# Low halves of projection weights made by accumulating DMAs, two tiles ahead, in a two-block transformer kernel

## Chip, cores and metric

The kernel runs on one core of a Trainium2 chip. The metric is the device time of one execution in microseconds (us). TensorE does the matrix products, ScalarE (ACT), VectorE (DVE) and GpSimd (POOL) the elementwise work, and SyncE (SP) issues the loads.

## What is computed

Two blocks work on one sequence of 256 frames of width 1024. The change lies in the RWKV-7 mixer of the second. Its three large projections take the mixed inputs through three 1024 x 1024 weight matrices in float32:

```python
xx = jnp.pad(h, ((0, 0), (1, 0), (0, 0)))[:, :-1] - h
xs = h[None] + xx[None] * mu[:, None, None, :]
rkv = jnp.einsum('pbtd,pde->pbte', xs[:3], w_rkv)
r, k, v = rkv[0], rkv[1], rkv[2]
...
y = _wkv7_scan(r_h, heads(decay), k_h, v_h, kk, kk * heads(a).astype(f32))
```

The scan is done in chunks: small Gram matrices of the decayed keys and receptances, a triangular elimination, and a chain of four windows.

## The kernel before

Every large product is made in three passes over split operands. A weight tile of 128 x 1024 numbers is cut by `split` into a high half (ACT copies it to fp32r) and a low half (the weight minus the high half). `mm3` then issues three matmuls, on L227, L228 and L229; the low half of the weight is first needed by the third of them for keys and receptance (L229) and by the second for values (L228).

```python
act.copy(hv, src)
lo.tensor_tensor(out=lv, in0=src, in1=hv.bitcast(F32), op=ALU.subtract)
```

The engine of the subtraction, `lo`, is DVE or POOL, by a string of letters in the table `KP` (`rk`, `rr`, `rv` for the key, receptance and value weights). There are 24 such tiles in the mixer: 8 of keys (`k_proj`, four calls, profile names wk, wkh, wkl), 8 of receptance (`r_proj`, wr, wrh, wrl) and 8 of value (`v_proj`, wv, wvh, wvl). Before, all 8 key tiles, 5 receptance tiles and 5 value tiles are subtracted on DVE, and 3 receptance and 3 value tiles on POOL.

Halves live in a pool `wp` of two buffers, raw weights in a pool `wr` of two buffers of 8 KB per partition. One load on SP brings a pair of key or receptance tiles (256 columns, 1 MB); value weights come 512 KB at a time. A load starts when its raw buffer is free, that is when both its tiles have been split; a split starts when the halves two tiles back have been used by TensorE.

The tile framework orders each engine's queue by its own estimate of when an instruction can run, and each engine works its queue in order. So in the profile some instructions stand earlier than in the code (the first key split runs while the layer before still multiplies).

In the mixer TensorE goes through the key projection with the low-rank products between (until 714 us of the span), two receptance calls, the normalisation of the keys (`scale_ab`, L1390 to L1401, with the small inverse square root of L284 to L282 ahead of it), 32 x 32 Gram blocks (`blocks`, L1458), and then a filler `dense()` that holds the rest of the receptance projection, the first half of the value projection, the large Gram matrices (`gram`, evicted by DVE in L1473) and transposes (`turn_bk`), while DVE and POOL run the elimination of 15 steps (L918, L921, L924) on two halves, POOL having the products of the second half (L921). From 791 us on TensorE alternates the rest of the value projection with the products that use the elimination's result.

Of the kernel before, what the change touches and what calls it, by code (L numbers as in the profile page):

```python
# [10 lines left out]
F32 = mybir.dt.float32  # L11
F32R = mybir.dt.float32r
I32 = mybir.dt.int32
AF = mybir.ActivationFunctionType
# [3 lines left out]
P = 128  # L18
# [42 lines left out]
def _pack(d):  # L61
# [46 lines left out]
    'pv': 3,  # L108
    'r3': 'p',
    'rho': 'd',  # L110
    'rk': 'dd,dd,dd,dd',
    'rr': 'dp,pd,dd,pd',
    'rv': 'd,d,d,p,d,d,p,p',
    'sev': 2,
    'sn': 'aapd',
    'srw': 5,
# [17 lines left out]
def tile_two_blocks(ctx: ExitStack, tc: tile.TileContext, a: dict):  # L134
# [1 line left out]
    act, dve, pool, pe, sync = nc.scalar, nc.vector, nc.gpsimd, nc.tensor, nc.sync  # L136

    cp = ctx.enter_context(tc.tile_pool(name="const", bufs=1))
    EN = {"d": dve, "p": pool, "a": act}

    def scale_by(e, out, in_, cols):
        if e is act:
# [35 lines left out]

    def raw(name):
        wpick[1] += 1  # L180
        w_ = extra[-1][1] if extra and wpick[1] % 2 and not wpick[2] else wr
        return w_.tile([P, 2048], F32, tag="raw", name=name)

    def load_ws(w, c0, name, n=256):
        t = raw(name)
        v = t[:, :NK * n].rearrange("p (k c) -> p k c", k=NK)
        sync.dma_start(out=v, in_=w[:, c0:c0 + n].rearrange("(k p) c -> p k c", p=P))
        return v
# [16 lines left out]
    def split(src, name, lo=dve, at=None):  # L205
        shape = list(src.shape)
        n = 1
        for s in shape[1:]:
            n *= s
        if at is None:  # L210
            wpick[0] += 1
            w_ = extra[-1][0] if extra and wpick[0] % 2 and not wpick[2] else wp
            h = w_.tile([P, 1024], F32R, tag="wh", name=name + "h")
            l = w_.tile([P, 1024], F32R, tag="wl", name=name + "l")
        else:
            x = area(at, [2, D], F32R)
            h, l = x[:, 0], x[:, 1]
        hv, lv = h[:, :n], l[:, :n]
        if len(shape) == 3:
            hv = hv.rearrange("p (a b) -> p a b", a=shape[1])  # L220
            lv = lv.rearrange("p (a b) -> p a b", a=shape[1])
        act.copy(hv, src)  # L222
        lo.tensor_tensor(out=lv, in0=src, in1=hv.bitcast(F32), op=ALU.subtract)  # L223
        return hv, lv

    def mm3(out, lh, ll, rh, rl, first, last):
# [916 lines left out]
    def rwkv(fed, early, cols, mu, hcol, hka, laf):  # L1143
        NP, CH = 8, 64
        half = 0.5 * DECAY
        with tc.tile_pool(name="rw", bufs=1) as bp:
            nkeep = _O2["reset2"][0]
            cc = bp.tile([P, nkeep], F32, tag="cc2", name="cc2")
            sync.dma_start(out=cc, in_=a["c2"][:, :nkeep])
# [41 lines left out]
            with tc.tile_pool(name="rwm2", bufs=2) as m2, tc.tile_pool(name="rwm", bufs=1) as mp:  # L1191
# [9 lines left out]
                xx = xxf.rearrange("p (k t) -> p k t", k=NK)  # L1201
                mixf = m2.tile([P, 2, 1024], F32, tag="mix", name="mix", bufs=1)
                sqf = m2.tile([P, 2, 512], F32, tag="sq", name="sq", bufs=1)
                w3 = a["rwkv_w_rkv_2"][0]

                xh, xl, _, part = fed
                pool.memset(hT[:, :, 0:1], 0.0)
# [78 lines left out]
                nk = mp.tile([P, 2, 2 * NP], F32, tag="nk", name="nk")  # L1286

                def k_proj(c, kh, kl):
                    w = load_ws(w3[1], c * 256, f"wk{c}")
                    hl = [split(w[:, :, j * P:(j + 1) * P], "wk", EN[KP["rk"].split(",")[c][j]]) for j in range(2)]  # L1290
                    q = lin("k")
                    qv = q.rearrange("p (j t) -> p j t", j=2)
                    if c == 0:
                        for i, j, k in [(i, j, k) for i in range(2) for j in range(2) for k in range(4 * i, 4 * i + 4)]:
                            mm3(qv[:, j], hl[j][0][:, k], hl[j][1][:, k], kh[:, k], kl[:, k],
                                (i, j, k) == (0, 0, 0), (i, j, k) == (1, 1, 7))
                    else:
                        for j in range(2):
                            ws(qv[:, j], *hl[j], kh, kl)
                    s = slice(2 * c, 2 * c + 2)  # L1300
                    act.copy(tK[:, s], as4(qv))
                    if KP["ka"][c] == "a":
                        for j in range(2):
                            act.activation(out=tA[:, 2 * c + j], in_=as2(qv)[:, j], func=AF.Copy,
                                           scale=cols[:, 64 + 2 * c + j:65 + 2 * c + j])
                    else:
                        dve.tensor_tensor(out=tA[:, s], in0=as2(qv), in1=cols[:, 64 + 2 * c:66 + 2 * c].unsqueeze(2)
                                          .unsqueeze(3).to_broadcast([P, 2, 2, P]), op=ALU.mult)
                    sq = sqf[:, c % 2].rearrange("p (j t) -> p j t", j=2)
                    act.activation(out=as2(sq), in_=tA[:, s], func=AF.Square)  # L1310
                    q = ps("kk")
                    for t in range(2):
                        for j in range(2):
                            pe.matmul(q[:, 4 * t + 2 * j:4 * t + 2 * j + 2], lhsT=sq[:, j, t * P:(t + 1) * P],
                                      rhs=cst("par"), start=True, stop=True)
                    dve.tensor_scalar(nk[:, :, 4 * c:4 * c + 4], q[:, :8].rearrange("p (t k) -> p t k", t=2),
                                      1e-24, RS, ALU.max, ALU.mult)
# [83 lines left out]
                    EN[KP["tk"][1]].tensor_tensor(out=tK[:, s], in0=tK[:, s], in1=as4(tt[:, s]), op=ALU.mult)  # L1401

                def r_proj(c):
                    w = load_ws(w3[0], c * 256, f"wr{c}")
                    q = lin("r")
                    qv = q.rearrange("p (j t) -> p j t", j=2)
                    for j in range(2):
                        wh, wl = split(w[:, :, j * P:(j + 1) * P], "wr", EN[KP["rr"].split(",")[c][j]])
                        for k in range(NK):
                            mm3(qv[:, j], wh[:, k], wl[:, k], rh[:, k], rl[:, k], k == 0, k == NK - 1)  # L1410
                            if k % 2:
                                yield 1
                    s = slice(2 * c, 2 * c + 2)
                    dve.tensor_mul(as4(pr[:, s]), as4(qv), tK[:, s])
                    dve.tensor_tensor(out=tR[:, s], in0=as4(qv), in1=EL5[:, s, :, :, 1:], op=ALU.mult)
                    EN[KP["tt"]].tensor_tensor(out=tK[:, s], in0=tK[:, s], in1=as4(EnL[:, s]), op=ALU.mult)
# [92 lines left out]
                def v_proj(n):  # L1509
                    ac = gv[2]  # L1510
                    m = slice(n * 512, n * 512 + 512)
                    for c in range(4):
                        w = raw(f"wv{n}{c}")[:, :1024].rearrange("p (k c) -> p k c", k=2)
                        sync.dma_start(out=w, in_=w3[2][c * 256:c * 256 + 256, m].rearrange("(k p) c -> p k c", p=P))
                        wh, wl = split(w, "wv", EN[KP["rv"].split(",")[4 * n + c]])
                        for j in range(2):
                            k = 2 * c + j
                            for t in range(2):
                                s = slice(t * P, t * P + P)
                                mm3(ac[t][:, m], vh[:, k, s], vl[:, k, s], wh[:, j], wl[:, j], k == 0, k == NK - 1)  # L1520
                                yield k, t
# [276 lines left out]
                    add_res(ac[1], 1, n, None)  # L1798
                for n in range(2):
                    fed[2](1, n)  # L1800
            return fed

    with more_weights(1, 1):
# [88 lines left out]
```

## Time and profile before

| | us |
|---|---|
| median of 3 runs | 1083.26 (1081.01 to 1083.73) |
| the profiled execution | 1082.76 |
| its span in the trace | 1081.0 |
| TensorE busy in the span | 1044.6 |
| DVE busy | 734.9 |
| ACT busy | 553.0 |
| POOL busy | 71.2 |

The profiled execution is 0.50 us under the median, and 1.76 us of it lie outside the span. Busy time of TensorE is modelled and matmuls overlap, so a busy TensorE is not one at its peak. In the rows below PE is TensorE's matmuls and PEld its weight loads; a wait is put down to the instruction that released it.

### The profile page before, as it was taken

What the parts mean: (1) busy time and instruction counts of PE and PEld (TensorE: products, weight loads), DVE (VectorE), ACT (ScalarE), POOL (GpSimd) and SP (SyncE); (2) the same over time, 40 slices, a digit from 0 to 9 for tenths busy, and PEclk for the clock granted to TensorE, in tenths of its full rate; (3) what the DMA queues carried; (4) which work ended last, traced back from release to release, by engine and by line L of the source; (5) the groups of instructions that cost most, each with busy time, mean ns of one, the idle gap of its engine ahead of it and who ended that gap; (6) DMA issues with size and microseconds to landing.
All of it is one profiled execution on the core that took longest, in us unless ns stands there. A gap on an engine that the chain in (4) does not pass through costs nothing.

```text
span 1081.0 us, 19651 instructions
## 1 busy us (share of the span) xinstructions
PE 1044.6 (97%) x8138; PEld 936.9 (87%) x8138; DVE 734.9 (68%) x1269; ACT 553.0 (51%) x826; POOL 71.2 (7%) x100
## 2 busy tenths in 40 slices
PE   8999999999999999999999999989999999999996
PEld 6899879988889999889999998989768869999985
DVE  5889675555568876676675556998954785555565
ACT  4745464454456454455554446852445645444452
POOL 3100000000002000000000001044320000000000
PEclk9999999999999999999999999998998999999999
DMA  8353196655564656555586541332133244665541
GB/s 245 122 157 118 45 343 196 195 162 189 160 211 139 215 157 194 160 172 185 156 273 194 179 154 47 98 105 92 60 99 112 86 156 158 193 195 187 187 133 40
DMA packets 113910, 169.44 MB, mean 157 GB/s; under 512 B 6446, under 2 KB 92443, under 8 KB 113564
## 3 DMA queue, kind: packets, MB, share of 16 engines
q1 hardware_dynamic: 113674, 168.11, 48.4%
q8 instruction: 64, 1.05, 0.4%
q14 instruction: 26, 0.21, 0.1%
q10 hardware_dynamic: 146, 0.07, 0.0%
HBM read 167.12 MB, written 1.05 MB: 156 GB/s over the span
## 4 chain that ended last, share of the span: by engine, by line
PE 82%; DVE 12%; ACT 3%; issue 2%; DMA 1%; POOL 1%; ACTq 0%; POOLq 0%; DVEq 0%
PE m1a L227 3%; PE m3h L228 3%; PE m3h L229 3%; PE m1a L229 3%; PE m1a L228 3%; PE m3h L227 3%; PE m1h L228 3%; PE m2h L228 3%; PE m2h L229 3%; PE m1h L229 3%; PE m1h L227 3%; PE m2h L227 3%; PE m2a L227 3%; PE m2a L228 3%; PE m2a L229 3%; PE m3a L227 3%
## 5 line engine op out<-in xcount | busy, mean ns | idle before, releaser
L227 PE MATMUL m1h<-m1xh,m1uh 128*128 128x256 f32 x256 | 73.4, 287 | 0.0
L229 PE MATMUL m3h<-m3xh,m3ul 128*128 128x256 f32 x256 | 72.3, 283 | 0.5 <-DVE m3ul L223 0.5
L228 PE MATMUL m3h<-m3xl,m3uh 128*128 128x256 f32 x256 | 72.2, 282 | 0.3 <-DVE m3xl L387 0.3
L227 PE MATMUL m3h<-m3xh,m3uh 128*128 128x256 f32 x256 | 72.1, 282 | 0.0
L228 PE MATMUL m1h<-m1xl,m1uh 128*128 128x256 f32 x256 | 71.9, 281 | 0.2 <-DVE m1xl L387 0.2
L229 PE MATMUL m2h<-m2xh,m2ul 128*128 128x256 f32 x256 | 71.7, 280 | 0.0
L229 PE MATMUL m1h<-m1xh,m1ul 128*128 128x256 f32 x256 | 71.7, 280 | 0.0
L228 PE MATMUL m2h<-m2xl,m2uh 128*128 128x256 f32 x256 | 71.7, 280 | 0.0
L223 DVE TENSOR_TENSOR m3ul<-m3u,m3uh 128x1024 fp32r<-128x1024 f32 x32 | 39.2, 1226 | 47.6 <-ACT m3uh L222 47.6
L227 PE MATMUL m2h<-m2xh,m2uh 128*128 128x256 f32 x256 | 71.6, 280 | 0.0
L223 DVE TENSOR_TENSOR m1ul<-m1u,m1uh 128x1024 fp32r<-128x1024 f32 x32 | 39.2, 1225 | 44.8 <-ACT m1uh L222 44.8
L223 DVE TENSOR_TENSOR m2ul<-m2u,m2uh 128x1024 fp32r<-128x1024 f32 x32 | 39.1, 1225 | 35.9 <-ACT m2uh L222 35.9
L222 ACT CAST m3uh<-m3u 128x1024 fp32r<-128x1024 f32 x32 | 33.5, 1047 | 53.9 <-PE m3h L228 50.0
L222 ACT CAST m1uh<-m1u 128x1024 fp32r<-128x1024 f32 x32 | 33.7, 1053 | 52.1 <-PE m1h L228 50.4
L222 ACT CAST m2uh<-m2u 128x1024 fp32r<-128x1024 f32 x32 | 33.5, 1050 | 47.9 <-PE m2h L228 45.4
L223 DVE TENSOR_TENSOR m2dl<-m2d,m2dh 128x1024 fp32r<-128x1024 f32 x32 | 39.2, 1224 | 26.1 <-ACT m2dh L222 26.1
L223 DVE TENSOR_TENSOR m3dl<-m3d,m3dh 128x1024 fp32r<-128x1024 f32 x31 | 38.0, 1225 | 24.9 <-ACT m3dh L222 24.9
L223 DVE TENSOR_TENSOR m1dl<-m1d,m1dh 128x1024 fp32r<-128x1024 f32 x31 | 37.9, 1224 | 22.0 <-ACT m1dh L222 22.0
L222 ACT CAST m2dh<-m2d 128x1024 fp32r<-128x1024 f32 x32 | 33.6, 1050 | 33.4 <-PE m2a L229 29.9
L222 ACT CAST m1dh<-m1d 128x1024 fp32r<-128x1024 f32 x31 | 32.5, 1047 | 35.3 <-PE m1a L229 24.4
L227 PE MATMUL m2a<-m2dh,m2fh 128*128 128x512 f32 x128 | 50.1, 391 | 0.0
L228 PE MATMUL m2a<-m2dl,m2fh 128*128 128x512 f32 x128 | 49.9, 390 | 0.0
(709 smaller groups left out, 3528.0 us busy)
## 6 DMA issues: line engine op xcount, KB each, us to landing
m1u<-in_w_up_dram SPq DMA_DIRECT2D x16, 1024.0 KB
m1d<-in_w_down_dram SPq DMA_DIRECT2D x16, 1024.0 KB, 4.9
m2u<-in_ffn_w_dram SPq DMA_DIRECT2D x16, 1024.0 KB, 6.6
m2d<-in_ffn_w_dram SPq DMA_DIRECT2D x16, 1024.0 KB, 5.6
m3u<-in_ffn_w_dram SPq DMA_DIRECT2D x16, 1024.0 KB, 5.6
m3d<-in_ffn_w_dram SPq DMA_DIRECT2D x16, 1024.0 KB, 4.8
win<-in_w_in_dram SPq DMA_DIRECT2D x10, 1024.0 KB
sv<-in_sgu_w_in_dram SPq DMA_DIRECT2D x8, 1024.0 KB, 6.9
```

What stands on the lines that cost most here:

```text
L222: act.copy(hv, src)
L223: lo.tensor_tensor(out=lv, in0=src, in1=hv.bitcast(F32), op=ALU.subtract)
L227: pe.matmul(out, lhsT=lh, rhs=rh, start=first, stop=False)
L228: pe.matmul(out, lhsT=lh, rhs=rl, start=False, stop=False)
L229: pe.matmul(out, lhsT=ll, rhs=rh, start=False, stop=last)
```

## The change

20 of the 24 weight tiles get the letter x. For them `split` no longer subtracts: ACT writes the high half, then ACT writes its negative into the low half's buffer, and POOL issues a DMA that adds the raw weights (SBUF to SBUF, 512 KB) onto it. The four key tiles of the first two calls stay on DVE. A second pool `wz` with two buffers for halves is opened around the mixer, so that halves alternate between four buffers, and `tile_of` makes each tile two tiles before TensorE uses it (one tile before in the first key call). Loads change in shape: key and receptance pairs come as two DMAs of 128 columns (512 KB each) into one raw buffer, value tiles as pairs in one load of 1 MB instead of two of 512 KB. The raw buffers stay two. The space that is reserved for descriptors of POOL's DMAs falls from the default to 1024 bytes per partition.

```diff
-    'rk': 'dd,dd,dd,dd',
-    'rr': 'dp,pd,dd,pd',
-    'rv': 'd,d,d,p,d,d,p,p',
+    'rk': 'dd,dd,xx,xx',
+    'rr': 'xx,xx,xx,xx',
+    'rv': 'x,x,x,x,x,x,x,x',
...
         act.copy(hv, src)
-        lo.tensor_tensor(out=lv, in0=src, in1=hv.bitcast(F32), op=ALU.subtract)
+        if lo == "x":
+            act.activation(out=lv, in_=hv.bitcast(F32), func=AF.Copy, scale=-1.0)
+            pool.dma_start(out=lv.bitcast(F32), in_=src, accum_op=ALU.add)
+        else:
+            lo.tensor_tensor(out=lv, in0=src, in1=hv.bitcast(F32), op=ALU.subtract)
...
+        with tc.tile_pool(name="wz", bufs=2) as wz, tc.tile_pool(name="rw", bufs=1) as bp:
+            extra.append((wz, None))
...
+            def prep(i):
+                if i > 23 or i in made:
+                    return
+                m, u = divmod(i, 8)
+                if u % 2 == 0:
+                    t = raw(f"w{'krv'[m]}{u}")
+                    if m < 2:
+                        v = t.rearrange("p (j k c) -> p j k c", j=2, k=NK)
+                        for j in range(2):
+                            sync.dma_start(out=v[:, j], in_=w3[1 - m][:, (u + j) * P:(u + j + 1) * P]
+                                           .rearrange("(k p) c -> p k c", p=P))
+                        src[i], src[i + 1] = v[:, 0], v[:, 1]
...
+                made[i] = split(src.pop(i), "w" + "krv"[m], EN[how[m][u]])
+
+            def tile_of(m, u, ahead=2):
+                for i in range(8 * m + u + ahead + 1):
+                    prep(i)
+                return made[8 * m + u]
...
-                    w = load_ws(w3[1], c * 256, f"wk{c}")
-                    hl = [split(w[:, :, j * P:(j + 1) * P], "wk", EN[KP["rk"].split(",")[c][j]]) for j in range(2)]
+                    hl = [tile_of(0, 2 * c + j, 2 if c else 1) for j in range(2)]
...
-                        wh, wl = split(w[:, :, j * P:(j + 1) * P], "wr", EN[KP["rr"].split(",")[c][j]])
+                        wh, wl = tile_of(1, 2 * c + j)
...
-                        wh, wl = split(w, "wv", EN[KP["rv"].split(",")[4 * n + c]])
+                        wh, wl = tile_of(2, 4 * n + c)
...
-    nc = bacc.Bacc("TRN2", target_bir_lowering=False, num_devices=1)
+    nc = bacc.Bacc("TRN2", target_bir_lowering=False, num_devices=1, dynamic_dma_scratch_size=1024)
```

## Rows read from the trace of the kernel before

**Rows 1.** Page, part 1: busy us (share of the span) and instructions of each engine
```profile
PE 1044.6 (97%) x8138; PEld 936.9 (87%) x8138; DVE 734.9 (68%) x1269; ACT 553.0 (51%) x826; POOL 71.2 (7%) x100
```

**Rows 2.** Stretches of 10 us: length, busy (instructions) by engine, clock, DMA share, GB/s
```profile
700.00:710.00 10.00, 9.19 (x66) 8.98 (x65) 10.00 (x17) 7.69 (x12) 4.15 (x3) 0.83 0.34 105
...
740.00:750.00 10.00, 8.66 (x88) 8.51 (x76) 9.96 (x19) 2.10 (x2) 8.02 (x6) 0.83 0.14 48
...
780.00:790.00 10.00, 9.29 (x56) 6.43 (x54) 9.44 (x25) 4.90 (x7) 1.22 (x2) 0.86 0.18 52
...
sum 120.00, PE 110.43 PEld 97.27 DVE 106.50 ACT 60.13 POOL 36.27; mean PE 9.20 PEld 8.11 DVE 8.88 ACT 5.01 POOL 3.02
```

**Rows 3.** Waits of PE, 690 to 800 us: us in total, times, longest
```profile
PE A L1469 <- DVE lx L1473: 2.4, 1, 2.4
PE nk L1394 <- ACT ly L1390: 1.6, 1, 1.6
PE AB L1458 <- issue: 1.3, 1, 1.3
PE v L227 <- DVE V L1529: 1.3, 2, 0.7
PE kk L1314 <- ACT sq L1310: 1.1, 1, 1.1
PE r L229 <- POOL wrl L223: 0.9, 1, 0.9
PE k L229 <- DVE wkl L223: 0.8, 1, 0.8
```

**Rows 4.** Groups by line, 690 to 800 us: busy us, mean ns, idle before
```profile
L223 DVE TENSOR_TENSOR wrl<-wr,wrh 128x1024 fp32r<-128x1024 f32 x5 | 6.7, 1336 | 0.0
L223 DVE TENSOR_TENSOR wvl<-wv,wvh 128x1024 fp32r<-128x1024 f32 x5 | 6.0, 1206 | 0.0
L223 DVE TENSOR_TENSOR wkl<-wk,wkh 128x1024 fp32r<-128x1024 f32 x4 | 4.8, 1212 | 0.0
...
L222 ACT CAST wrh<-wr 128x1024 fp32r<-128x1024 f32 x8 | 8.4, 1046 | 16.4 <-PE r L228 12.9 <-PE k L228 3.5
...
L223 POOL TENSOR_TENSOR wvl<-wv,wvh 128x1024 fp32r<-128x1024 f32 x3 | 7.2, 2413 | 7.8 <-ACT wvh L222 7.8
L223 POOL TENSOR_TENSOR wrl<-wr,wrh 128x1024 fp32r<-128x1024 f32 x3 | 7.1, 2369 | 11.8 <-ACT wrh L222 6.5 <-PE AB L1458 5.3
```

**Rows 5.** Timeline of DVE and of POOL around 720 us: start, us, instruction
```profile
720.08 2.31 DVE L275 TENSOR_TENSOR nt<-nr 128x32 f32<-128x32 f32 x1
...
723.10 0.19 DVE L275 TENSOR_TENSOR nt<-nr 128x32 f32<-128x32 f32 x1
...
719.97 2.38 POOL L223 TENSOR_TENSOR wrl<-wr,wrh 128x1024 fp32r<-128x1024 f32 x1
```

**Rows 6.** Groups by line of DVE, 690 to 800 us, two that POOL's neighbourhood touches
```profile
L1369 DVE TENSOR_SCALAR lx<-lv,hka 128x256 f32<-128x256 f32 x7 | 4.3, 679 | 0.0
...
L1574 DVE TENSOR_TENSOR hT<-xx,cc 128x512 f32<-128x512 f32 x2 | 3.5, 1769 | 0.0
```

**Rows 7.** DMA view: loads of these weights, count, KB each, us to landing
```profile
wk<-in_rwkv_w_rkv_dram SPq DMA_DIRECT2D x4, 1024.0 KB, 5.1
wr<-in_rwkv_w_rkv_dram SPq DMA_DIRECT2D x4, 1024.0 KB, 6.3
wv<-in_rwkv_w_rkv_dram SPq DMA_DIRECT2D x8, 512.0 KB, 3.9
```

**Rows 8.** Tile views: matmuls with a low half, ns min/median/max, first and last start
```profile
L229 PE MATMUL k<-mkh,wkl x64: 277/280/420, 678.6 to 714.1; 128*128 128x256 f32 x64
...
L229 PE MATMUL r<-mrh,wrl x64: 277/281/514, 714.4 to 756.2; 128*128 128x256 f32 x64
...
L228 PE MATMUL v<-wvl,mvh x32: 387/396/628, 756.5 to 807.7; 128*128 128x512 f32 x32
```

**Rows 9.** Groups by line of POOL, 690 to 800 us: the elimination's products
```profile
L921 POOL TENSOR_TENSOR elp<-elb,hT 128x16 f32<-128x16 f32 (+14 forms) x15 | 8.4, 557 | 24.1 <-DVE elb L918 17.2 <-DVE elp L921 6.0 <-DVE hT L924 0.9
```

More of the change, by code (lines that the diff above doesn't have):

```diff
@@ L138, in tile_two_blocks @@
     cp = ctx.enter_context(tc.tile_pool(name="const", bufs=1))
-    EN = {"d": dve, "p": pool, "a": act}
+    EN = {"d": dve, "p": pool, "a": act, "x": "x"}
     def scale_by(e, out, in_, cols):
@@ L180, in raw @@
         wpick[1] += 1
-        w_ = extra[-1][1] if extra and wpick[1] % 2 and not wpick[2] else wr
+        w_ = extra[-1][1] if extra and extra[-1][1] and wpick[1] % 2 and not wpick[2] else wr
         return w_.tile([P, 2048], F32, tag="raw", name=name)
@@ L1145, in rwkv @@
         half = 0.5 * DECAY
-        with tc.tile_pool(name="rw", bufs=1) as bp:
+        with tc.tile_pool(name="wz", bufs=2) as wz, tc.tile_pool(name="rw", bufs=1) as bp:
+            extra.append((wz, None))
+            w3 = a["rwkv_w_rkv_2"][0]
+            made, src = {}, {}
+            how = [KP[x].replace(",", "") for x in ("rk", "rr", "rv")]
+            def prep(i):
[10 more added lines that the diff above has]
+                        src[i], src[i + 1] = v[:, 0], v[:, 1]
+                    else:
+                        v = t.rearrange("p (j k c) -> p j k c", j=2, k=2)
+                        n, c = divmod(u, 4)
+                        sync.dma_start(out=t.rearrange("p (k c) -> p k c", k=4),
+                                       in_=w3[2][c * 256:c * 256 + 512, n * 512:n * 512 + 512]
+                                       .rearrange("(k p) c -> p k c", p=P))
+                        src[i], src[i + 1] = v[:, 0], v[:, 1]
+                made[i] = split(src.pop(i), "w" + "krv"[m], EN[how[m][u]])
[3 more added lines that the diff above has]
+                return made[8 * m + u]
             nkeep = _O2["reset2"][0]
@@ L1203, in rwkv @@
                 sqf = m2.tile([P, 2, 512], F32, tag="sq", name="sq", bufs=1)
-                w3 = a["rwkv_w_rkv_2"][0]
                 xh, xl, _, part = fed
@@ L1403, in r_proj @@
                 def r_proj(c):
-                    w = load_ws(w3[0], c * 256, f"wr{c}")
                     q = lin("r")
@@ L1512, in v_proj @@
                     for c in range(4):
-                        w = raw(f"wv{n}{c}")[:, :1024].rearrange("p (k c) -> p k c", k=2)
-                        sync.dma_start(out=w, in_=w3[2][c * 256:c * 256 + 256, m].rearrange("(k p) c -> p k c", p=P))
-                        wh, wl = split(w, "wv", EN[KP["rv"].split(",")[4 * n + c]])
+                        wh, wl = tile_of(2, 4 * n + c)
                         for j in range(2):
@@ L1800, in rwkv @@
                     fed[2](1, n)
+            extra.pop()
             return fed
```

## The prediction, made before the changed kernel was run

> **What bounds the kernel now.** I read the shares of the engines first: TensorE is busy for 1044.6 of 1081.0 us [rows 1]. Its products are all still there after the change, so a gain can only come from stretches in which it waits or runs slowly. The table by stages finds them. In the 120 us from 680 on, DVE is busy for 106.5 us, more than in any other long stretch, while PE loses 9.6 us (120.0 less 110.4) and the granted clock is not full in five of twelve slices: 0.83 at 700 and 740 us, 0.86 at 780 [rows 2]; the slice at 750 repeats the 0.83, and the one at 770 has 0.97. The reader is to see two things: the part that the change works on is the part where DVE, not TensorE, sets the pace, and it is a ninth of the span.
>
> The list of PE's waits there says what a freer DVE is worth: seven lines, 9.4 us [rows 3]. In five DVE or POOL stands behind the wait at first or second hand: the Gram products that wait for an eviction, 2.4; `nk`, which waits for ACT, which waits for the inverse square root on DVE, 1.6; the value product for V, 1.3; a low half from POOL, 0.9; one from DVE, 0.8. `kk` waits for ACT's squares, which wait for a DVE product queued behind a weight subtraction, 1.1. The last, 1.3 us of "issue" at the Gram blocks, has no releaser, and I leave it standing. So 8.1 us can go.
>
> **What the change takes away.** On DVE 14 subtractions: 4 of keys, 5 of receptance, 5 of values, 4.8 + 6.7 + 6.0 = 17.5 us [rows 4]. On POOL six, 7.2 + 7.1 = 14.3 us [rows 4]. These cost DVE more than their place in POOL's queue: while POOL subtracts from 719.97 to 722.35, a DVE product of 128x32 numbers takes 2.31 us, and the same form takes 0.19 at 723.10 [rows 5]. The two products of L1574 have a mean of 1769 ns [rows 6]; the one that stands beside a POOL subtraction takes 2.85, the other 0.69. There are four such stretched spots: 0.9 (an L1270 of 2.1 against 1.2), 2.1, 2.2 and 2.4 (a pair of L924 in the elimination, 3.05 against some 0.6), in sum 7.6 us. DVE is thus relieved of 17.5 + 7.6 = 25 us of the 106.5, about 22 of them before 791 us. PE cannot use that much: the bound of the gain is PE's own lost time, 8.1 us.
>
> **What it adds on ACT.** 20 negations of 128x1024. The nearest row is the cast of the same size, 1046 ns [rows 4], so 21 us, laid on an ACT that is busy for 60.1 of 120 [rows 2]. The room is there after 720 us; in 680 to 710 ACT is already near 8 of 10 us per slice, and 4 to 6 negations fall there, as well as high halves that are now made earlier. What waits behind them in ACT's queue is tanh and exp of the decay, which DVE's scans need. I count nothing, since DVE gets 4.8 us back in the same place, and keep 2 us for the range.
>
> **What it adds on POOL and in the queues.** 20 DMA issues. No DMA of POOL's stands in the trace, so its price has bounds only. For POOL's own time: below, 0.2 us, a small DVE product; above, 2.4 us, the subtraction it replaces [rows 4, 5]. I take 1.0, between them, since issuing reads no tile. For the transfer: below, the 3.9 us in which 512 KB of value weights land; above, the 6.3 us of a 1 MB load, because an accumulation reads two operands [rows 7]. I take 5. The Trainium skill, "DMA: Bandwidth & Descriptors" (section Anatomy of one DMA), gives 2.0 us plus the bytes over 436 GB/s for a DMA issued by GpSimd, an estimate of 3.2 us for 512 KB; this trace has 3.9 us for a load of SP's, and by the page's figure the chain below would be 1.8 us shorter.
>
> A low half is then there 1.05 + 1.05 + 1.0 + 5 = 8.1 us after its split can start (6.2 to 10.8 by the bounds), where a DVE subtraction took 2.3. Is that hidden? With four buffers and work two tiles ahead, a split can start when the tile four back is used, so three tiles of TensorE's time are left. At its bare pace, 24 matmuls that start 0.118 us apart in the timeline (each lasts some 280 ns [rows 8], but they overlap) make 2.8 us a tile: 8.5 us. That is just enough, and in the receptance and value stretches a tile takes longer, as other products stand between.
>
> The raw buffers are the tighter loop. SP's next load waits until both accumulations have read the buffer: landing 5.1 to 6.3, four ACT passes 4.2, issue and transfer 4.1 to 8.7, in all 13.4 to 19.2 us for each of two buffers, or 6.7 to 9.6 per pair of tiles, 8.3 with my values. Before, keys took (714.1 - 678.6)/4 = 8.9 us per pair, receptance 10.5, values 12.8 [rows 8]. So the loop holds in the fillers and is at its edge for the last keys and the first receptance tiles. I charge 2.5 us there: one wait of about 1 us for the first accumulated key tile and two of some 0.75 behind it. The loads of 128 columns have rows of 512 B instead of 1 KB; the trace has no such load to price, and I count it within the 5.1 to 6.3.
>
> **The sum.** 1082.76 (profiled execution) - 8.1 + 2.5 = 1077.2 us; against the median, which lies 0.5 higher, 1077.7, so 1078. From 791 us on I change nothing: there PE alternates between value tiles and the solver's products.
>
> **Rivals.**
> *The clock comes back too.* The three slices of [rows 2] and the one at 750 us grant 0.83, 0.83, 0.86 and 0.83, which is 6.5 us of full-speed time. Three of them follow a wait of 1.1, 1.3 or 2.4 us. If such waits bring the slow level, taking them away gives up to 6.5 more: 1071. Against it: the slices from 720 to 740 hold waits of 0.9 and 1.6 and grant 1.00.
> *Nothing is won.* POOL has 15 elimination products, which form a chain with DVE's [rows 9]. Seven accumulating DMAs fall in that stretch. POOL works in order, so each trigger that waits for ACT's negation (1 to 2 us) and then issues (1.0) holds the next product. At 0.8 us a step for seven that is 5.6 us on a chain which was to win 3.7 (2.4 at the Gram eviction and 1.3 at V); with the 2.5 above the gain is used up: 1083. For it: POOL's only stretch of use is this. Against: POOL idles 24.1 us before those products [rows 9].
> *A trigger is starved.* The Trainium skill, "SBUF — State Buffer" (section Who interferes with whom), says that DVE copies and tensor-scalar instructions in a two-port mode block GpSimd's descriptor writing entirely; no run here shows it yet. In this kernel the place would be the DVE tensor-scalars of L1369, 4.3 us nearly in one run [rows 6], just where the last key tiles need their DMA. A trigger 4 us late there delays one key tile by so much: 1082.
> *Slower.* The accumulation is much slower than a load. From 9.5 us of transfer on, the loop, (6.3 + 4.2 + 1 + 9.5)/2, passes the 10.5 us of a receptance pair [rows 8]. At 12 us it is 11.8 per pair: two key pairs lose 2.9 each and four receptance pairs 1.3 each, 11 us, against 6.4 of gains that remain (8.1 less the two waits for low halves): 1082.8 + 11 - 6.4 = 1087.4, with the first tile's wait 1088. For it: each such DMA moves 512 KB twice in and once out beside loads that already keep the DMA engines at 0.14 to 0.34 [rows 2]. Against: it needs over twice the value load's 3.9 us.
>
> **How the numbers follow.** My forecast 0.45 (its own range 1074 to 1081), clock as well 0.10, nothing won 0.15, starved trigger 0.05, slower 0.25. A measurement of this kernel tells 0.3%, 3.2 us, from no change: faster is under 1080.0, slower over 1086.5. Faster: most of the forecast and the clock case, 0.48; slower: most of the slow case and a little of the second, 0.27; same: 0.25. The range runs from half of the clock's return to a transfer of some 14 us: 1070 to 1092.
>
> **What would show it.** Right: the seven waits of [rows 3] are gone but for the one at AB; DVE falls by about 25 us and ACT rises by about 21; no DVE product of 128x32 takes 2 us; the elimination ends 3 to 5 us earlier. Wrong: L229 (k, r) or L228 (v) waits for a DMA in more than three places; SP's weight loads wait for DMAs and not for DVE; POOL's L921 waits for ACT; the landing time of an accumulation is over 9 us.

## The result, and the profile after

The changed kernel takes 1088.85 us (median of four runs, 1088.0 to 1089.9) against 1082.76 for the kernel before: a ratio of 1.0056, interval 1.004 to 1.0072. It is slower by 6.1 us, where 1078 was forecast. Its profiled execution took 1088.0 us with a span of 1085.9, 4.9 us longer than the span before.

Page of the changed kernel, part 1, to be read beside [rows 1]:

```profile
PE 1050.5 (97%) x8138; PEld 941.6 (87%) x8138; DVE 712.1 (66%) x1255; ACT 571.5 (53%) x846; POOL 70.7 (7%) x114
```

DVE is relieved by 22.8 us and ACT has 18.5 more, near the 25 and 21 of the working; POOL is unchanged. TensorE has the same 8138 products and needs 5.9 us more for them.

Groups by line of the changed kernel, 690 to 800 us (busy, mean ns, idle before), the work that replaces the subtractions of [rows 4]:

```profile
L224 ACT ACTIVATE wvl<-wvh 128x1024 fp32r<-128x1024 f32 x8 | 8.4, 1056 | 0.2
L224 ACT ACTIVATE wrl<-wrh 128x1024 fp32r<-128x1024 f32 x8 | 8.3, 1049 | 0.0
L225 POOL DMA_DIRECT2D wvl<-wv x8 | 7.0, 878 | 16.6 <-ACT wvl L224 16.4 <-issue 0.2
L225 POOL DMA_DIRECT2D wrl<-wr x8 | 7.0, 874 | 15.9 <-ACT wrl L224 12.0 <-DVE nk L1349 2.5 <-PE nk L1427 1.4
```

The transfers, in the DMA view from 660 to 800 us (count, KB each, us to landing) and the spread that the tile views add for wkl, wrl and wvl, in this order:

```profile
wkl<-wk POOLq DMA_DIRECT2D x4, 512.0 KB, 5.2
wrl<-wr POOLq DMA_DIRECT2D x8, 512.0 KB, 5.5
wvl<-wv POOLq DMA_DIRECT2D x8, 512.0 KB, 6.6
```

```profile
DMA to landing us min/median/max: 4.6/5.2/5.8
DMA to landing us min/median/max: 4.5/5.5/8.0
DMA to landing us min/median/max: 4.5/6.6/9.8
```

A negation costs what the cast costs, 1.05 us; an issue holds POOL 0.88 us; an accumulation lands after 4.5 to 9.8 us.

Waits of PE in the changed kernel, 690 to 800 us (total, times, longest), against [rows 3]:

```profile
PE AB L1490 <- issue: 2.0, 1, 2.0
PE r L233 <- DMA wrl<-wr: 1.9, 2, 1.6
PE A L1501 <- DVE lx L1505: 1.3, 2, 0.9
PE kk L1347 <- ACT sq L1343: 1.0, 1, 1.0
PE A L1501 <- DVE lv L1505: 0.5, 1, 0.5
PE nk L1427 <- ACT ly L1423: 0.3, 1, 0.3
```

They come to 7.0 us, 2.4 less than before. The waits for V and for the two subtractions are gone; the Gram eviction still costs 1.8 of 2.4, `nk` 0.3 of 1.6. So the change does win something here, and the loss stands elsewhere. In this execution a part of it is found in the table by stages: first the kernel before, then the changed one (length, busy by engine, granted clock, DMA share, GB/s).

```profile
690.00:740.00 50.00, 45.42 (x582) 43.33 (x583) 47.72 (x77) 28.80 (x43) 13.89 (x9) 0.97 0.33 104
740.00:790.00 50.00, 45.59 (x339) 38.06 (x326) 46.04 (x136) 18.74 (x37) 18.97 (x21) 0.90 0.23 74
820.00:860.00 40.00, 37.67 (x607) 34.23 (x600) 20.97 (x49) 26.96 (x47) 1.05 (x1) 0.87 0.26 87
```

```profile
690.00:740.00 50.00, 46.76 (x538) 44.85 (x538) 32.78 (x61) 36.23 (x52) 15.55 (x16) 0.93 0.87 200
740.00:790.00 50.00, 46.18 (x377) 38.44 (x363) 37.71 (x134) 26.61 (x48) 19.29 (x28) 0.83 0.73 170
820.00:860.00 40.00, 37.85 (x632) 34.24 (x626) 20.44 (x45) 26.15 (x45) 1.04 (x1) 0.83 0.26 88
```

TensorE is busier in each of these stretches, but at a lower granted clock: a mean of stretches at full speed (2.4 GHz) and at half (1.2 GHz). Length times (1 - clock) is the time lost against full speed if TensorE works all the while: 1.5 + 5.0 + 5.2 = 11.7 us before, 3.5 + 8.5 + 6.8 = 18.8 after. These 7.1 us are an upper bound, because a low clock during a wait costs nothing. They are more than the span's whole 4.9, but this is one execution: a second profile of the same kernel (e16, below) has a span of 1085.7 us and loses 11.7 us in these three stages, as the kernel before. So the place of the low clock is not fixed by the program.

The elimination did get faster. Its result on one half (`xx`, on DVE) and the first product that uses it (`Pc`, on PE), before and then after:

```profile
789.46 0.68 DVE L1584 TENSOR_TENSOR xx<-hT,cc 128x512 f32<-128x512 f32 x1
791.69 1.02 PE L1591 MATMUL Pc<-xx 32*32 32x32 f32 x96
```

```profile
783.25 0.68 DVE L1614 TENSOR_TENSOR xx<-hT,cc 128x512 f32<-128x512 f32 x1
790.82 0.75 PE L1621 MATMUL Pc<-xx 32*32 32x32 f32 x64
```

The result is there 6.2 us earlier, and TensorE comes to it 0.9 us earlier: it is still busy with the filler. DVE's chain does not set the pace there.

The last reading is at the end of the mixer, which the prediction left out. PE's waits of the changed kernel from 850 to 890 us (first line); then two lines of its DVE timeline, the low half of the next MLP's first weight and the norm's last product that stands behind it; then that low half in the kernel before:

```profile
PE yt L252 <- DVE tBK L1740: 2.0, 1, 2.0
```

```profile
872.75 1.22 DVE L227 TENSOR_TENSOR m3ul<-m3u,m3uh 128x1024 fp32r<-128x1024 f32 x1
...
877.98 0.68 DVE L1740 TENSOR_TENSOR tBK<-tBK,V 128x512 f32<-128x512 f32 x1
```

```profile
878.55 1.23 DVE L223 TENSOR_TENSOR m3ul<-m3u,m3uh 128x1024 fp32r<-128x1024 f32 x1 [0.31 <-ACT m3uh L222]
```

The second pool of halves is open until the mixer ends, so the halves of w_out go to it by turns, the buffer for m3u is free earlier, and this subtraction, which stood behind the norm's products, now stands ahead of the small inverse square root that they need. The wait before the third transpose of y is 2.0 us instead of 0.4.

### The profile page after: what moved, and what is told of

Its sections match the earlier page's. It is cut to its first block, busy times and chain, and to the rows that moved or that the text cites. A ratio compares the mean times of both kernels' runs of the same rounds, so it can differ in the third digit from the quotient of the medians.

```text
span 1085.9 us, 19709 instructions
## 1 busy us (share of the span) xinstructions
PE 1050.5 (97%) x8138; PEld 941.6 (87%) x8138; DVE 712.1 (66%) x1255; ACT 571.5 (53%) x846; POOL 70.7 (7%) x114
## 3 DMA queue, kind: packets, MB, share of 16 engines
q8 instruction: 64, 1.05, 0.4%
HBM read 167.12 MB, written 1.05 MB: 155 GB/s over the span
## 4 chain that ended last, share of the span: by engine, by line
PE 82%; DVE 9%; issue 3%; ACT 3%; DMA 2%; POOL 1%; POOLq 0%; ACTq 0%; DVEq 0%
PE m1a L231 3%; PE m3h L232 3%; PE m3h L233 3%; PE m1a L233 3%; PE m1a L232 3%; PE m3h L231 3%; PE m1h L232 3%; PE m2h L232 3%; PE m2h L233 3%; PE m1h L233 3%; PE m2h L231 3%; PE m1h L231 3%; PE m2a L231 3%; PE m2a L232 3%; PE m2a L233 3%
## 5 line engine op out<-in xcount | busy, mean ns | idle before, releaser
L222 ACT CAST m3dh<-m3d 128x1024 fp32r<-128x1024 f32 x31 | 32.7, 1054 | 33.4 <-PE m3a L233 31.6
```

## The experiments

Theory A: the loss comes from late accumulations (TensorE waits for them, or raw buffers are held by them). Theory B: it comes from the structure around them, that is four buffers, two tiles ahead and the new loads, through the order of the queues. Later theory C: the granted clock takes back what DVE's relief gives (in e2's expectation C is the negations on ACT). "Letters" are the strings of `KP`. All ratios are against runs of the kernel before on the same chip; the last column is the mean granted clock over the timed executions.

| | median us | ratio | interval | clock |
|---|---|---|---|---|
| kernel before | 1082.1 to 1083.3 | 1 | | 0.987 to 0.988 |
| e1_pipe_only | 1094.2 | 1.0098 | 1.0075 to 1.0122 | 0.978 |
| e2_neg_add | 1087.15 | 1.0034 | 1.0019 to 1.0048 | 0.985 |
| e3_v_only | 1086.05 | 1.0034 | 1.0019 to 1.005 | 0.982 |
| e4_kr_only | 1091.38 | 1.0086 | 1.0068 to 1.0104 | 0.979 |
| e5_early_close | 1084.84 | 1.0018 | 1.0003 to 1.0034 | 0.983 |
| e6_not_ahead | 1090.5 | 1.0053 | 1.0037 to 1.0069 | 0.982 |
| e7_dma_not_ahead | 1098.91 | 1.0139 | 1.0125 to 1.0152 | 0.978 |
| e8_before_no_pool | 1082.73 | 0.9993 | 0.9983 to 1.0002 | 0.987 |
| e9_early_close_no_dma | 1091.02 | 1.0071 | 1.0056 to 1.0086 | 0.980 |
| e10_early_close_v | 1083.99 | 1.0022 | 1.0003 to 1.004 | 0.983 |
| e11_v_alone_old_order | 1093.35 | 1.0096 | 1.0076 to 1.0116 | 0.981 |
| e12_first_r_on_dve | 1085.23 | 1.0023 | 1.0008 to 1.0038 | 0.983 |
| e13_before_bon_spread | 1082.46 | 0.9991 | 0.9975 to 1.0006 | 0.987 |
| e14_early_close_bon_spread | 1089.97 | 1.0055 | 1.0035 to 1.0075 | 0.983 |
| e15_early_close_v_bon_spread | 1083.2 | 1.0001 | 0.9982 to 1.0021 | 0.985 |
| e16_changed_again | 1088.73 | 1.006 | 1.0044 to 1.0076 | 0.981 |
| e17_early_close_again | 1087.78 | 1.0055 | 1.0041 to 1.007 | 0.981 |

**The structure without its DMAs (e1).**

```diff
-    'rk': 'dd,dd,xx,xx',
-    'rr': 'xx,xx,xx,xx',
-    'rv': 'x,x,x,x,x,x,x,x',
+    'rk': 'dd,dd,dd,dd',
+    'rr': 'dp,pd,dd,pd',
+    'rv': 'd,d,d,p,d,d,p,p',
```

> The new structure (tiles two ahead, four buffers of halves, loads of 128 columns, value pairs) with all 24 low halves subtracted on DVE and POOL as before; no accumulating DMA, no negation. Theory A (the accumulations are late: raw buffers are held, the loads queue behind them, TensorE waits and then runs at the lower clock): without them the loss goes, 1079 to 1083 us. Theory B (the structure and the new order of the queues that comes with it cost, not the DMAs): the loss stays, 1086 to 1090 us.

1094.2 us, 5 us slower than the changed kernel. Theory A falls as the cause of the loss: without any accumulation the loss is larger. The changed kernel is about 5 us faster than e1, but e2 shows that this need not be the work of its DMAs. One cost of the structure is seen in DVE's timeline of e1, of which the weight subtractions and four steps of the inverse square root are shown (left out between them: other products):

```profile
722.65 1.22 DVE L227 TENSOR_TENSOR wrl<-wr,wrh 128x1024 fp32r<-128x1024 f32 x1
723.79 0.17 DVE L288 TENSOR_SCALAR nr<-nk 128x32 int32<-128x32 int32 x1
...
726.05 0.18 DVE L279 TENSOR_TENSOR nt<-nr 128x32 f32<-128x32 f32 x1
...
726.75 0.80 DVE L280 TENSOR_TENSOR nt<-nt,nk 128x32 f32<-128x32 f32 x1
727.47 1.21 DVE L227 TENSOR_TENSOR wrl<-wr,wrh 128x1024 fp32r<-128x1024 f32 x1
```

Receptance subtractions that are ready early stand before and inside the chain that `scale_ab` and so the Gram blocks need. In this profile the cost is small: from the first key product to the last of the solver's third set (`Rc`, L1613 before and L1643 here) e1 takes 142.8 us and the kernel before 141.7. The profiled execution (1090.09) is the fastest of e1's four, so it does not show all of the loss.

**The accumulation done by DVE (e2).** The negations stay on ACT; DVE adds the raw weights.

```diff
-            pool.dma_start(out=lv.bitcast(F32), in_=src, accum_op=ALU.add)
+            dve.tensor_tensor(out=lv, in0=src, in1=lv.bitcast(F32), op=ALU.add)
```

> As the changed kernel with the 20 negations on ACT, but DVE adds the raw weights onto them (20 x 1.2 us) and no DMA accumulates. Theory A: the DMA was the cost, so 1080 to 1084 us, though DVE has 24 us again. Theory B: 1086 to 1090. A third theory C (the negations fill ACT's queue and hold tanh, exp and the high halves): also 1086 to 1090, while the kernel without negations is fast.

1087.15 us: DVE's adds cost no more than the DMAs that replace them, within their intervals. So putting some 24 us of work back on DVE is not seen in the time: the relief of DVE, on which the prediction rests, is worth nothing that these runs can measure. And e2 is 7 us faster than e1 without any DMA; it has the negations and none of POOL's subtractions, and which of these counts was not run. PE waits 1.8 us for a wrl of DVE's where it waited 1.9 for one of the DMA's, and 3.6 for V.

**Accumulating DMAs on a part (e3, e4).** e3 keeps them on the eight value tiles and e4 on keys and receptance; the others have the letters of before.

> Accumulating DMAs for the eight value tiles alone; keys and receptance are subtracted as before, within the new structure. Theory A: value tiles have 12.8 us per pair, more than the loop of the raw buffers needs, so nothing is lost and DVE's relief in the elimination shows: 1078 to 1082 us. Theory B: 1085 to 1089 us.

> Accumulating DMAs for four key and eight receptance tiles alone; values are subtracted as before. Theory A: here the loop is at its edge, so most of the loss is here: 1086 to 1090 us. Theory B: no different from value tiles alone, 1085 to 1089 us.

1086.05 and 1091.38 us. Beside the bare structure (1094.2) the time is 8 us less with the value tiles' DMAs and 3 less with those of keys and receptance; they do not add up (together 5), and e2 has 7 without a DMA. In e4 PE waits 3.3 us for V again, which e3 does not have.

**The second pool closed earlier (e5, e9, e10).** The line moves ahead of the products with w_out; e9 has the letters of before, e10 has x on value tiles only.

```diff
                 for _ in late_fill:
                     pass
+                extra.pop()
                 yh, yl = xt_tiles("y")
...
-            extra.pop()
             return fed
```

> The changed kernel, with one line moved: the second pool of halves is taken out of use right after the value projection, before the products with w_out, instead of at the end of the mixer. All 20 accumulating DMAs and the work two tiles ahead stay. Theory B (the loss lies in the order of the queues that the new structure brings, in two places): in the changed kernel the low half of the next MLP's first weight (m3ul on DVE) stands ahead of the norm chain because the halves of w_out go partly to the second pool; with the line moved this place is as before, TensorE's wait for tBK at the third yt falls from 2.0 to about 0.5 us, and the time is 1.6 to 3 us under the changed kernel: 1086 to 1087. Theory A (what is lost comes from late accumulations, up to 810 us): nothing after the mixer's value projection matters, 1088.9. Either way it stays slower than the kernel before (1082.5), since some 3 us are lost before 863 us.

> The structure without accumulating DMAs (the letters of the kernel before, as in the run that took 1094.2), now with the second pool closed right after the value projection. If the early close is worth a constant at the end of the mixer (4.0 us in the changed kernel), this gives 1090; the DMAs are then worth 1090 - 1084.8 = 5 us beside the same structure, as they were with the late close (1094.2 - 1088.85 = 5.3). If the two interact, the difference comes out elsewhere than 4 to 7 us.

> Accumulating DMAs on the eight value tiles alone, keys and receptance with the letters of before, two tiles ahead and four buffers for all 24, second pool closed early. With the late close it took 1086.05. If the early close gives 4.0 again: 1082, level with the kernel before. If its gain is smaller, since this variant's profile lost less at the end: 1084.

1084.84, 1091.02 and 1083.99 us: 4.0, 3.2 and 2.1 less than with the late close, which was measured in another session. The wait before the third transpose is 0.5 us again in e5. But e5 ran from 1081.68 (clock 0.986) to 1090.14 (0.979), and e10 from 1079.45 (0.987) to 1090.77 (0.978), so these medians hold a second thing; e16 and e17 come back to it.

**Nothing made ahead (e6 with the letters of before, e7 with x).**

```diff
-            def tile_of(m, u, ahead=2):
+            def tile_of(m, u, ahead=0):
...
-                    hl = [tile_of(0, 2 * c + j, 2 if c else 1) for j in range(2)]
+                    hl = [tile_of(0, 2 * c + j) for j in range(2)]
```

> The new structure without its DMAs and without the work ahead: four buffers for the halves and the new shape of loads, but each tile is made when TensorE's code comes to it, and the low halves are subtractions on DVE and POOL by the letters of the kernel before. Beside the structure with the work two tiles ahead and the same letters, which took 1094.2. Theory B1 (it is the place in the code, two tiles ahead, that puts weight subtractions ahead of the inverse square root in DVE's queue): most of the loss goes, 1084 to 1087, with the 1.6 us of the m3ul place left in it. Theory B2 (it is the four buffers, which let a split start earlier whatever its place in the code): it stays at 1092 to 1095. Theory B3 (the loads of 128 columns): also 1092 to 1095, but with TensorE waiting for wkh or wrh from late loads. Theory A has nothing to say here, since no DMA accumulates.

> The changed kernel with all its 20 accumulating DMAs, but each tile is made when TensorE's code comes to it, not two ahead; four buffers stay. Theory A (the chain of a low half, cast, negation, issue and transfer, some 8 us, must be hidden, and the work ahead hides it): TensorE now waits for DMAs at most of the 20 tiles, 1 to 3 us each, 1100 or more. Theory B1 (the queue orders each engine by its own estimate of readiness, so that four buffers alone let the splits start early, and the place in the code only decides ties): 1086 to 1090, near the changed kernel, and any gain over it is what the work ahead cost in order.

e6: 1090.5, between the forecasts of B1 and B2. The work ahead is 3.7 us of e1's loss (4.9 by the ratios), and the rest stays with the four buffers, the new loads and the late close. e7: 1098.91. Waits of PE in e7, 690 to 800 us:

```profile
PE r L232 <- issue: 5.0, 1, 5.0
PE r L233 <- DMA wrl<-wr: 4.6, 2, 2.6
PE kk L1347 <- ACT sq L1343: 3.3, 2, 2.0
PE k L233 <- DMA wkl<-wk: 2.2, 2, 1.4
```

Here theory A's mechanism is real, at four places (6.8 us) and not at most of the 20 tiles: the chain of a low half is long and must be hidden. The two tiles of lead that cost 3.7 us without DMAs are what makes the DMAs usable.

**POOL's subtractions by themselves (e8).** The kernel before, with p replaced by d in `rr` and `rv`.

> The kernel before with one change: the six subtractions of POOL are done by DVE. It measures by itself a term of the prediction, the DVE products that are stretched while POOL subtracts (7.6 us in four places), against the time that DVE then needs for six more subtractions (6 x 1.2 = 7.3 us). If the stretched products are a cost on the path, as the prediction took them, the two cancel: 1081 to 1084. If DVE's own load sets the pace and the stretch is mostly hidden: 1085 to 1090.

1082.73 us, no difference. The product of [rows 5] that took 2.31 us takes 0.18 here and L1574 [rows 6] falls from 3.5 to 2.5, but six subtractions come to DVE for it. The stretched products were real, and worth no more than the 7 us of subtractions that DVE then has more.

**Value tiles alone, in the old order (e11).** Keys and receptance as in the kernel before; value tiles by DMA, two ahead, the first two made beside the last two receptance tiles; second pool from there to the end of the value projection.

```diff
                         wh, wl = split(w[:, :, j * P:(j + 1) * P], "wr", EN[KP["rr"].split(",")[c][j]])
+                        if c == 3:
+                            vtile(j - 2)
...
-                        wh, wl = split(w, "wv", EN[KP["rv"].split(",")[4 * n + c]])
+                        wh, wl = vtile(4 * n + c)
```

> The kernel before for keys and receptance (its loads, its letters, two buffers, nothing ahead), and only the eight value tiles by accumulating DMA, two tiles ahead, in four buffers that exist from the last two receptance tiles to the end of the value projection. Theory B (the loss is in the order of the queues around keys and receptance and at the end of the mixer; the DMAs by themselves win where DVE has no room): nothing before 745 us changes, TensorE's waits for V (1.3) and for the Gram eviction (2.4) shrink, and the time is 1079 to 1082, the first version that beats the kernel before. Theory C (the clock and the chain of the elimination take back what the DMAs free): 1082 to 1086. Theory A (late accumulations): a wait of L228 for a DMA at each of several value tiles, 1086 or more.

1093.35 us: theory B in its pure form falls too. Two lines of PE's waits of e11 (670 to 830 us) and POOL's timeline:

```profile
PE v L231 <- DVE V L1553: 4.6, 1, 4.6
PE v L232 <- DMA wvl<-wv: 3.9, 1, 3.9
```

```profile
749.43 1.32 POOL L1442 TENSOR_TENSOR tBK<-tBK,lv 128x512 f32<-128x512 f32 x1
751.69 1.18 POOL L925 TENSOR_TENSOR elp<-elb,hT 128x32 f32<-128x32 f32 x1 [0.94 <-DVE hT L928]
752.82 1.04 POOL L225 DMA_DIRECT2D wvl<-wv  x1
```

ACT's negation was done at 749.1, but its trigger stands in POOL's queue behind a product of `turn_bk` and one of the elimination, which waits for DVE. It goes out 3.7 us late, and TensorE meets it at 761.5 us with 3.9 us of wait.

**The first receptance pair on DVE (e12).** e5 with `'rr': 'dd,xx,xx,xx'`.

> The changed kernel with the second pool closed early and the first two receptance tiles subtracted on DVE, so that 18 DMAs accumulate. It takes away the only waits of TensorE for an accumulation that the profiles show (2.2 us at two places, first receptance tiles). If these waits are on the path: 1084.8 - 2 = 1083, or 1081 if the slow clock behind them goes too. If the wait is only passed on, because the products behind it (AB, which waits for issue 2.0 to 3.2 us) wait for other things: 1084 to 1085.5. If the two subtractions go ahead of the inverse square root in DVE's queue, as without DMAs: 1086 or more.

1085.23 us, as e5. The waits for an accumulation fall from 2.2 us in e5 to 1.1, and the wait of AB for issue grows from 3.2 to 4.6: it is only passed on.

**Narrow products spread (e13 before, e14 on e5, e15 on e10).** Twelve of the 16 bonus products stand between products of the last receptance tiles.

```diff
-                    for c in (2, 3):
-                        yield from r_proj(c)
+                    yield from r_proj(2)
                     q2 = ps("bon")
...
+                    for k, y in enumerate(r_proj(3)):
+                        if k < 6:
+                            bons(k)
+                        yield y
```

> The kernel before with one change in the order of TensorE's code: twelve of the sixteen narrow bonus products (128x2, two for each of eight tiles, in the trace before one run of 2.7 us at 749 and one of 1.0 at 757) stand between the wide products of the last receptance tile, and only the last four in a run. Nothing accumulates. If a run of narrow products brings the slow granted clock (before: 0.54 and 0.61 from 752 to 756, just behind the first run), one slow episode of some 1.7 us of full-speed time goes: 1080 to 1081. If the slow clock there has another origin: 1081.5 to 1083.

> The changed kernel with the second pool closed early and the same spreading of the bonus products. In the changed kernel's profile the clock is at its low level from 754 to 765, behind bonus products that stand in a bunch from 753.4 to 756.6 and 758.7 to 760.6. If they bring it: 1 to 3 us less than the early close alone (1084.84), 1082 to 1084, and fewer executions above 1086. If not: 1084 to 1086, with slow slices in the same places.

> Accumulating DMAs on the value tiles alone, early close, and the bonus products spread. The same kernel without the spreading took 1083.99, from 1079.45 at a mean granted clock of 0.987 to 1090.77 at 0.978. If the clock is what divides its executions and the bunch of narrow products is what brings it: 1081 to 1082.5, near or below the kernel before. If the clock goes its own way: 1083 to 1085 with the same scatter.

Windows of the kernel before, then of e13:

```profile
744.00:748.00 4.00, 4.00 (x30) 4.00 (x30) 3.96 (x10) 1.05 (x1) 3.17 (x3) 0.83 0.00 0
752.00:756.00 4.00, 4.00 (x22) 3.94 (x21) 1.89 (x15) 0.00 (x0) 0.86 (x3) 0.57 0.70 228
```

```profile
744.00:748.00 4.00, 4.00 (x20) 4.00 (x20) 2.89 (x9) 0.82 (x1) 1.99 (x2) 0.50 0.00 0
752.00:756.00 4.00, 4.00 (x34) 3.86 (x33) 2.29 (x11) 1.05 (x1) 0.69 (x2) 1.00 0.43 138
```

The low stretch behind the run of narrow products is gone, in e14 and e15 too. But the one behind the wait at AB (1.3 us before, 1.9 in e13) is longer, and the time does not fall: 1082.46, 1089.97 (5 more than e5), 1083.2 us. e14 shows why one place does not decide: a wait of 2.7 us for V is back, and from 820 to 838 us the granted clock is 0.50 throughout, the lower of the two levels (1.2 GHz).

**Changed kernel and early close side by side (e16, e17).**

> The changed kernel itself, unaltered, beside the one with the early close on one chip and beside the same runs of the kernel before. Its four executions so far lie at 1088.0 to 1089.9, all at a mean granted clock of 0.981 or 0.982; the early close has the same order of every queue up to the end of the mixer and ran from 1081.68 to 1090.14 at 0.979 to 0.986. If the late close costs only what the profile shows at the end of the mixer (1.6 us) and the clock scatters in both alike, this comes out at 1086 to 1087 with a scatter of 6 to 9 us, and 1.0 to 2.5 us over its sibling. If it costs 4 us by itself: 1088 to 1089, 3 to 5 over the sibling.

> The early close beside the changed kernel, on the same chip. By the first hypothesis 1084 to 1086, 1.0 to 2.5 us under the sibling; by the second 1084 to 1085, 3 to 5 under it.

1088.73 and 1087.78 us on one chip. The medians differ by 1.0 us, but each kernel's six executions scatter over 4 to 5 us, so they do not tell 1 from 3; both are above the first hypothesis's level. The traces say more. The transposes of y, in the kernel before, the changed kernel, e16 and e17 (first and last start):

```profile
L248 PE MATMUL yt<-ident,tBK x16: 269/273/328, 860.1 to 878.8; 128*128 128x128 f32 x16
L252 PE MATMUL yt<-ident,tBK x16: 271/272/327, 863.1 to 882.2; 128*128 128x128 f32 x16
L252 PE MATMUL yt<-ident,tBK x16: 272/296/421, 860.7 to 880.9; 128*128 128x128 f32 x16
L252 PE MATMUL yt<-ident,tBK x16: 272/273/328, 864.9 to 883.6; 128*128 128x128 f32 x16
```

From the first of them to the end of the span it is 220.9, 222.8, 225.0 and 220.9 us. In all eight traces with the second pool open to the end (changed kernel, e1 to e4, e6, e7, e16) this stretch takes 222.7 to 225.0 us, and in the other eleven 220.8 to 221.2. So the late close costs 1.8 to 4.1 us. The 1.8 are waits. In the four that take 225 (e1, e2, e4, e16) the clock is low as well, behind the wait of 2.0 us: 0.91 from 860 to 900 us in e16, where the changed kernel's first profile has 1.00 behind the same wait. The stages of e16, to be held against the table of the changed kernel:

```profile
690.00:740.00 50.00, 46.58 (x480) 44.83 (x480) 33.52 (x63) 37.79 (x55) 15.65 (x15) 0.97 0.88 195
740.00:790.00 50.00, 45.48 (x487) 37.64 (x470) 42.66 (x138) 28.74 (x50) 19.52 (x28) 0.90 0.80 187
820.00:860.00 40.00, 37.47 (x611) 33.82 (x604) 20.70 (x46) 26.83 (x48) 1.04 (x1) 0.87 0.26 90
860.00:900.00 40.00, 35.66 (x190) 28.65 (x189) 28.40 (x73) 17.45 (x35) 0.00 (x0) 0.91 0.38 131
```

Up to the first transpose of y the traces of the changed kernel, e16, e5 and e17 have the same instructions in the same order on every engine, so they are four executions of one program. Their spans are made up of (us, from the first and last starts in the tile views):

| | before | changed | e16 | e5 | e17 |
|---|---|---|---|---|---|
| until the first key product | 678.4 | 678.3 | 680.9 | 680.4 | 682.5 |
| from there to the last `Rc` product | 141.7 | 143.2 | 139.5 | 139.7 | 141.3 |
| lost to the low clock from 690 to 820 us | 6.5 | 12.0 | 6.5 | 6.5 | 8.5 |
| from there to the first transpose of y | 40.0 | 41.6 | 40.3 | 40.2 | 41.1 |
| from there to the end | 220.9 | 222.8 | 225.0 | 221.0 | 220.9 |

With the same loss to the clock (e16, e5) the changed stretch is 2.0 to 2.2 us shorter than before: that is what the change wins. With 5.5 us more of it (the first profile) the same instructions take 3.7 us longer, some 0.7 us for each us lost. The first row differs by 4 us, for the most part in code that no edit touches: the granted clock of the first 200 us is 1.00, 1.00, 0.98, 0.98 and 0.97. The medians of e5 and e17, one program, differ in the same way: 1084.84 at a mean clock of 0.983, 1087.78 at 0.981.

No version is shown faster than the kernel before; e8, e13 and e15 equal it.

## Why the prediction was wrong

**The step that failed** is "The sum": it took 5.6 us off up to 791 us, put everything behind at nothing and left the granted clock where it was. The runs show in its place: 2.0 to 2.2 us won up to 820 us at the same clock (e16 and e5 against the kernel before); 1.8 to 4.1 us lost at the end of the mixer; and a lower clock. The rival "The clock comes back too" had the clock as a gain only; that it could fall further stood nowhere. The changed kernel has a mean clock of 0.981 over ten executions, the kernel before 0.987 to 0.988 in every batch: some 7 us more are lost against full speed. At 0.7 us for each that is some 5 us, an estimate from the two profiles of one kernel; the scatter within the changed kernel and within each of the seventeen versions (141 executions) agrees, with 0.8 us for 0.001 of clock. With the 1.8 of waits at the end, less the 2.1 won, and 0.3 us more outside the span (2.1 against 1.8) this is 5 of the 6.1 us measured.

**"DVE, not TensorE, sets the pace"** is the premise under it. It held at single waits only: the elimination's result came 6.2 us earlier and TensorE used 0.9 of that, and e2, with all 24 subtractions or adds on DVE, is no slower than the changed kernel.

**"So 8.1 us can go"** was too high. Of the six waits behind these 8.1 us 3.1 remain (kk 1.0, Gram 1.8, nk 0.3), so 5.0 went. Where the Gram products wait, DVE is as full as before (9.44 of 10 between 770 and 780 us, 9.41 before).

**"I charge 2.5 us"** for new waits was right in size, 1.9 us for two receptance tiles and 0.7 more at AB, and only in part in place: no key tile waits, though the first was charged 1 us. e12 shows that halving the first of these gains nothing.

**"From 791 us on I change nothing"** is wrong by 1.8 to 4.1 us (the stretch behind the first transpose of y).

So by the tables of waits 2.4 us go by 800 us and 1.6 come back at the end, a net gain of 0.8 us where the sum had 5.6.

**The terms.** DVE 22.8 us against 25. ACT 18.5 against 21. POOL's issue 0.88 us against 1.0. Transfer 5.2 to 6.6 us in the medians against 5. The Trainium skill, "DMA: Bandwidth & Descriptors" (section Anatomy of one DMA), gave an estimate of 3.2 us; no accumulation landed under 4.5. The chain of a low half is so 1.05 + 1.05 + 0.88 + 5.2 to 6.6 = 8.2 to 9.6 us, against 8.1. "DVE is thus relieved" counted 7.6 us for stretched products, and e8 gives them no value on the path.

**The rivals.** "Slower" has the time (1088) by luck and not the mechanism. Its signs are partly there: SP's loads do wait for accumulations (27.4 us for L1568's in the table of waits) and one landed after 9.8 us; but TensorE's 1.9 us of waits for them and e1 say that this is not what the time is made of. "Nothing is won" is not seen: POOL's elimination products wait for DVE (14.5 us for `elb`) and none for ACT, and the elimination ends earlier. e11 has its mirror image, a trigger held by the elimination. "A trigger is starved": POOL's issues waited 0.2 us for nothing visible in 19. The rule of the Trainium skill, "SBUF — State Buffer" (section Who interferes with whom), on descriptor writing that is blocked has no trace here; the triggers' idle time has ACT's negation, `nk` or a load behind it.

**The signs.** "No DVE product of 128x32 takes 2 us": right. "The elimination ends 3 to 5 us earlier": it ends 6 us earlier, but that sign was taken for a gain, and the first product that uses it starts at 790.8 instead of 791.7 us. "The seven waits are gone but for the one at AB": wrong, three more remain in part. Of the signs of being wrong, two came: SP's loads wait for accumulations, and one landing of 20 is over 9 us.

**What stays open.** Why the clock is lower. Its mean is 0.978 to 0.985 in every version with the second pool and 0.987 in the kernel before, e8 and e13, so it goes with the structure (e1 has 0.978 without any DMA) and not with DVE's or POOL's load. One place is shown by experiment: a low clock behind the first transposes of y comes only with the wait that the late close brings, in four of eight traces and in none of the eleven others. Elsewhere it is argued from the places only. The changed kernel's slice of 0.83 at 720 us stands behind a wait of 1.6 for wrl, and e5 has the same wait and 1.00 there; e12 to e15 moved such causes and the low stretches turned up elsewhere. Every version with the second pool also has the smaller space for descriptors, which was not run by itself; the clock of the first 200 us is 0.97 to 1.00 in these sixteen traces and 0.99 or 1.00 in the three without, too few to tell. Why four buffers and the new loads alone (e6) cost some 5 us beyond the late close's 1.8 is not taken apart either.

## What to carry to other kernels

An accumulating DMA can take a subtraction off a full engine, but here it needed some 9 us of lead, and the lead (more buffers, earlier code) reorders every queue that it passes: measure the structure alone, and the structure with the work back on the engine, before crediting the DMA. A chain that ends earlier wins only what the engine behind it can use: look where that engine stands when the result is there. A pool that stays open longer than its use changes the turns of the buffers, and with them the order of queues far behind the edit. When waits shrink and the time grows, set the granted clock of both profiles side by side, stretch by stretch, and the mean clock of many executions beside it, before looking for a new wait; and profile the same kernel twice, since two executions of equal span lost their clock in different stages here.

## What was unexpected of the hardware

The same program lies between 1079.45 and 1090.77 us (e10), at mean granted clocks of 0.987 and 0.978, where the kernel before stays within 3 to 5 us in all batches but one. The clock fell behind waits of 1.3 to 2.0 us and behind a run of narrow products of 2.7 us (0.57 for 4 us), but not each time: behind one wait of 2.0 us in four traces of eight. Accumulations of equal size landed after 4.5 to 9.8 us in stretches of 10 us in which the DMA share was 0.49 to 1.06.
